# Three edits to a decoder step built from seven-product matmuls: the last four pairs in turns, a norm in single steps, one more weight in flight

## The chip, the cores and the metric

The kernel runs on one core of a Trainium2 chip. The metric is device time in microseconds (us) of one execution. Engines: TensorE (PE; PEld is its weight load), VectorE (DVE), ScalarE (ACT), GpSimd (POOL) and SyncE (SP), which here only issues DMAs.

## The reference

One step of a two-layer decoder, 1,024 prompt positions and 8 single decode positions, width 2048, all in float32. The first layer is a pooling mixer, the second an attention over a window of 128 with shared keys and values. Cut to what matters:

```
def pool_layer(x, ...):                          # layer A
    z = x @ w_in                                 # stage ai: 2048 x 4096
    u, gate = z[..., :D_POOL], z[..., D_POOL:]
    d = grouped_linear(multiscale_pool(u)) * scale
    y = (d * silu(gate)) @ w_out                 # stage ao: 2048 x 2048
    return layer_norm(ALPHA * x + y, g_ln, b_ln)

k, v = shared_kv(h, pos, w_kv)                   # 2048 x 512, from the output of A

def attn_layer(x, ...):                          # layer B
    z = x @ w_in                                 # stage bi: queries and gate, 2048 x 4096
    o = attn_core(rope(q), kb, vb, ..., sinks)   # 32 heads of 64, 4 key/value heads
    y = (o * silu(gate)) @ w_out                 # stage bo: 2048 x 2048
    return layer_norm(ALPHA * x + y, g_ln, b_ln)
```

`layer_norm` takes mean and variance over the 2048 channels of each position.

## The kernel before, in words

Channels lie on the partitions (16 tiles of 128) and positions along the free dimension. The positions are cut into two chunks, the first of 512, the second of 512 + 8 = 520. Each of the four matmuls is run for both chunks, so there are eight stages: ai 0, ai 1, ao 0, ao 1, bi 0, bi 1, bo 0, bo 1 (the table `PHASES`). The sixth is bi 1, which begins with the keys and values of the second chunk; the eighth and last is bo 1, from about 2107 us to 2296 us.

Nearly all matmul work is done in *pairs* of output tiles. A pair is a 2 x 2 block product and takes seven products in place of eight (`seven`), so a stage of 2048 outputs has 8 pairs and 56 products. Each product is 8 steps over the contraction with three matmuls each (lines 684 to 686): a float32 operand is split into a high and a low part, and high x high, high x low and low x high are summed. A product needs one combined weight of 128 x 1024. It is loaded by SP (L285, 512 KB), cast to its high part by ScalarE (L505), and its low part is what VectorE subtracts (L520). The activations go the same way (L828 load, L838 cast, L847 subtraction). Behind each product VectorE or ScalarE takes the sums out of PSUM (L623 to L657).

The order of instructions on an engine is the order in which Python issues them. `begin`, ahead of each product, loads, prepares and casts the weights that lie `self.ahead` products ahead (three numbers: loads, casts, subtractions); `at(n, go)` puts a step behind the n-th product from now; `product(n, ...)` does that for extra matmuls. Side work, such as a norm, is a generator in `self.side`; `end` runs its next step once in `self.every` products if at least `self.room` tiles are free. All tiles come from one pool of 54 (`Mem`); a load into a tile waits for whatever used it before, and SP issues strictly in order.

Names in the prediction: `ln_gen` is the norm of a finished chunk as side work. In the eighth stage it is the last norm of the first chunk (output `y0`): two J sums (matmuls with a constant matrix that add over channels, L952), then for each of the 8 pairs a load (L994), a subtraction of the mean (L1068), a multiplication (L1069), two affine steps on ScalarE (L1060) and a store (L1061). In the sixth stage's transition, L1728 are four transfers that bring partner rows for the rotation, and L657 copies the last product out of PSUM to free it.

`phase_end` is the end of the last stage. The pairs named in `SPLIT` are not worked one behind the other but in turns, product by product, as the table `TAIL` says; `steps` lists what is done behind which product. The second chunk is halved in positions: Bh (260 columns) has its sums of squares and its statistics (`stats`) before the last product, A after it. For each pair, `less` and `rest` build the residual, `square` and `add` feed the sums, `affine1` (L1474, L1478 on VectorE) and `affine2` (L1485 on ScalarE, L1486 the store, output `y1`) finish a half pair, and `back` loads a pair that had been put away. Half A is finished in another way: `turn` transposes the unfinished pairs (L1588), the mean and bias come in as a small matmul (`last_rows`, L1596), and `evict` scales by the row's factor (L1608 on VectorE, L1613 on ScalarE) and stores (L1609, output `y1a`). `sums_a` (L1533) and `sums_z` (L1541) are the final sums, the second of the last pair alone.

Of the kernel before, what the change touches and what calls it, by code (L numbers as in the profile page):

```python
# [66 lines left out]
SPLIT = 5, 6, 7  # L67
TAIL = (
    (5, 0), (5, 2), (5, 1), (6, 0), (5, 3), (5, 4), (6, 2), (6, 1), (7, 0), (6, 3), (7, 2), (7, 1), (6, 4),
    (7, 3), (7, 4), (5, 5), (5, 6), (6, 5), (6, 6), (7, 5), (7, 6),  # L70
# [120 lines left out]
class Kern:  # L191
# [789 lines left out]
    def ln_gen(self, c, pre, acc, gc, bc, out, td):  # L981
# [81 lines left out]
        for p in range(10):  # L1063
            load(p + 2)
            if p < 8:
                t = self.pair_view(pre[p], T)
                if c == 0:
                    nc.vector.tensor_sub(t, t, b2(mu))  # L1068
                nc.vector.tensor_mul(t, t, b2(rr))  # L1069
# [334 lines left out]
    def phase_end(self, c, xs, x_in, pre, acc, gc, bc, out):  # L1404
# [30 lines left out]

        def square(p, h, j=slice(0, 2)):
            if p not in q:
                q[p] = self.mem.full(2 * T)
            nc.scalar.activation(self.pair_view(q[p], T)[:, j, h], tv(p)[:, j, h], AF.Square)

        def add(p, h):
            nc.vector.tensor_add(av[:, :, h], av[:, :, h], tv(p)[:, :, h])
            nc.vector.tensor_add(qv[:, :, h], qv[:, :, h], self.pair_view(q[p], T)[:, :, h])

        def sums(h):
# [3 lines left out]
            for ps, a, w in zip(R[h.start], (av, qv), (tv(z), self.pair_view(q[z], T))):  # L1449
                srcs = [v[:, j, h] for v in (a, w) for j in range(2)]  # L1450
# [3 lines left out]
        def stats(h):  # L1454
# [4 lines left out]
            nc.scalar.copy(m, mb[:, :TH])  # L1459
            nc.vector.tensor_mul(qq, m, m)  # L1460
# [76 lines left out]
        def sums_z(n):  # L1537

            w = (tv(z), self.pair_view(q[z], T))[n]
            for j in range(2):  # L1540
                nc.tensor.matmul(  # L1541
                    R[0][n][:, :TH], J, w[:, j, A], start=False, stop=j == 1, skip_group_check=True,
                )

        def moments():
# [15 lines left out]
            affine1a(1, Bh)  # L1561
# [7 lines left out]
            affine1b(1, Bh)  # L1569
# [32 lines left out]
        def evict(b, k):  # L1602
# [3 lines left out]
            r = box["rc"][:, b : b + 1]  # L1606
            if k % 2:
                nc.vector.tensor_scalar(y, X[b, k][:], r, None, op0=ALU.mult)  # L1608
# [3 lines left out]
            else:  # L1612
                nc.scalar.activation(y, X[b, k][:], AF.Copy, scale=r)  # L1613
# [13 lines left out]
        x, y, z = SPLIT  # L1627
        for p in SPLIT:
            box, z0, z1 = self.two(T)

            def open_(p=p, box=box, z0=z0):
# [6 lines left out]
            (x, 0): [lambda: x_in(y)],  # L1638
            (x, 2): [lambda: less(x)],
            (y, 0): [lambda: x_in(z)],  # L1640
# [22 lines left out]
            (z, 5): [lambda: square(y, A), lambda: affine(x, Bh), lambda: spare(4), lambda: scale(4)],  # L1663
            (z, 6): [
                lambda: square(z, A, 0), lambda: add(y, A), lambda: scale(z, (0,), True),
            ],
        }
        for p, idx in TAIL:
            for go in steps.get((p, idx), []):
                self.at(0, go)  # L1670
            if (p, idx) == (x, 5):
# [13 lines left out]
        scale(y)  # L1685
        spare(y)
        spare(z)
        affine1(z, Bh)
# [25 lines left out]
        affine1(3, Bh)  # L1714
        affine2(2, Bh)
# [766 lines left out]
```

## Time and profile before

| | |
|---|---|
| median of 3 runs | 2322.99 us (2320.79 to 2325.85) |
| profiled execution | 2320.17 us |
| its span, first to last instruction | 2317.9 us |
| TensorE busy | 2288.1 us, 99% |
| VectorE, ScalarE, GpSimd busy | 84%, 60%, 8% |
| mean granted TensorE clock | 0.997 |
| HBM traffic over the span | 275 GB/s |

The profiled execution takes 2.3 us outside its span. The page gives the busy time of each engine, groups of instructions by line, and the chain of work that ended last; the trace behind it answers what an engine waited for and what each did in any stretch. A releaser named behind an idle time is inferred, and of several it is the one that came last.

### The profile page before, as it was taken

The numbers are of one execution on the slowest core, as the hardware profiler recorded it, in microseconds if no ns is written. First come the engines' busy times: TensorE is split into PE (matmuls) and PEld (weight loads), VectorE is DVE, ScalarE is ACT, GpSimd is POOL, SyncE is SP. The second block draws the span as 40 slices with busy tenths as digits, with TensorE's granted clock in tenths as the row PEclk, the third lists the DMA queues.
The fourth block names the chain that finished last, engine by engine and source line by source line (L and its number), as shares of the span: only waits on it lengthen the run. The fifth ranks groups of instructions, "written<-read, shape, count | busy, mean of one in ns | idle before, by whom it ended". The sixth has DMA issues, their size and how long they took to land. (4 is left out here: it accounts for less than half of the span.)

```text
span 2317.9 us, 50529 instructions
## 1 busy us (share of the span) xinstructions
PE 2288.1 (99%) x20417; PEld 2217.7 (96%) x20417; DVE 1943.0 (84%) x2409; ACT 1389.3 (60%) x2548; POOL 191.1 (8%) x360
## 2 busy tenths in 40 slices
PE   9999999999999999999999999999999999999997
PEld 7999999999999999999889999989999999999997
DVE  8888889877878878988979898889877777889797
ACT  5544446544546547655566767685776678556565
POOL 0111110010000000000001111100000000000001
PEclk9999999999999999999999999999999999999999
DMA  7869679999989989999767666777787878799795
GB/s 261 287 242 315 229 245 330 315 309 303 304 302 322 335 284 333 317 392 345 245 234 241 233 234 236 252 259 250 234 252 240 252 230 288 251 360 381 252 330 184
DMA packets 246682, 649.37 MB, mean 280 GB/s; under 512 B 25232, under 2 KB 106032, under 8 KB 246448
## 3 DMA queue, kind: packets, MB, share of 16 engines
q1 hardware_dynamic: 204432, 493.66, 63.8%
q0 software_dynamic: 42016, 152.49, 17.0%
q8 instruction: 159, 2.61, 0.5%
q14 instruction: 75, 0.61, 0.1%
HBM read 463.54 MB, written 173.01 MB: 275 GB/s over the span
## 5 line engine op out<-in xcount | busy, mean ns | idle before, releaser
L684 PE MATMUL pD<-m,m 128*128 128x260 f32 (+1 forms) x5088 | 1441.3, 283 | 4.7 <-ACT pD L623 2.3
L686 PE MATMUL pD<-m,m 128*128 128x260 f32 (+1 forms) x5088 | 1434.7, 282 | 4.9 <-DVE m L520 4.9
L685 PE MATMUL pD<-m,m 128*128 128x260 f32 (+1 forms) x5088 | 1434.7, 282 | 0.0
L684 PEld LDWEIGHTS pD<-m,m 128*128 128x128 f32 x5088 | 959.4, 189 | 13.9 <-issue 6.2
L686 PEld LDWEIGHTS pD<-m,m 128*128 128x128 f32 x5088 | 959.8, 189 | 7.1 <-DVE m L520 7.0
L685 PEld LDWEIGHTS pD<-m,m 128*128 128x128 f32 x5088 | 959.1, 189 | 0.5
L520 DVE TENSOR_TENSOR m<-m,m 128x1024 fp32r<-128x1024 f32 x690 | 833.5, 1218 | 94.7 <-ACT m L505 44.1
L505 ACT CAST m<-m 128x1024 fp32r<-128x1024 f32 x690 | 720.5, 1049 | 249.9 <-DVE m L349 120.3
L349 DVE TENSOR_TENSOR m<-m,m 128x1024 f32<-128x1024 f32 x136 | 166.1, 1222 | 10.2 <-DMA m<-in_wia 5.7
L847 DVE TENSOR_TENSOR m<-m,m 128x1024 fp32r<-128x1024 f32 (+1 forms) x118 | 143.8, 1224 | 7.4 <-ACT m L838 5.8
L838 ACT CAST m<-m 128x1024 fp32r<-128x1024 f32 (+1 forms) x118 | 123.3, 1051 | 11.8 <-DVE m L520 3.5
L657 ACT COPY m<-pD 128x260 f32<-128x260 f32 (+1 forms) x89 | 33.2, 373 | 131.0 <-PE pD L686 131.0
L645 DVE TENSOR_TENSOR m<-pD,m 128x260 f32<-128x260 f32 (+1 forms) x92 | 38.4, 418 | 73.1 <-ACT pD L644 67.2
L1910 ACT ACTIVATE m<-m,sm 128x128 f32<-128x128 f32 x256 | 99.4, 392 | 0.0
L623 ACT ACTIVATE pD<-pD 128x260 f32<-128x260 f32 (+1 forms) x90 | 33.3, 370 | 102.2 <-PE pD L686 102.0
L1179 PE MATMUL pD<-m,m 128*128 128x260 f32 (+1 forms) x528 | 91.5, 323 | 0.0
L712 PE MATMUL pD<-m,m 128*128 128x512 f32 x224 | 89.1, 398 | 0.0
L714 PE MATMUL pD<-m,m 128*128 128x512 f32 x224 | 88.2, 394 | 0.0
L713 PE MATMUL pD<-m,m 128*128 128x512 f32 x224 | 88.1, 393 | 0.0
L1179 PEld LDWEIGHTS pD<-m,m 128*128 128x128 f32 x528 | 79.4, 188 | 8.2
L1923 ACT ACTIVATE m<-m,sm 128x128 f32<-128x128 f32 x256 | 81.8, 391 | 3.8 <-DVE sm L1918 3.4
L632 ACT COPY m<-pD 128x260 f32<-128x260 f32 (+1 forms) x92 | 34.3, 373 | 82.3 <-PE pD L686 82.0
(257 smaller groups left out, 2101.3 us busy)
## 6 DMA issues: line engine op xcount, KB each, us to landing
m<-in_wib SPq DMA_DIRECT2D x132, 512.0 KB
m<-in_wia SPq DMA_DIRECT2D x128, 512.0 KB
m<-swoa SPq DMA_DIRECT2D x64, 512.0 KB
swia<-m POOLq DMA_DIRECT2D x56, 512.0 KB, 4.9
m<-swia SPq DMA_DIRECT2D x56, 512.0 KB
m<-swob SPq DMA_DIRECT2D x56, 512.0 KB
m<-in_wob SPq DMA_DIRECT2D x52, 512.0 KB
m<-in_woa SPq DMA_DIRECT2D x48, 512.0 KB
```

Of the source, the lines that this page charges most:

```text
L349: self.nc.vector.tensor_add(s[out].a[:, :1024], s[x].a[:, :1024], s[y].a[:, :1024])
L505: self.nc.scalar.copy(hi.r[:, :1024], self.stream[self.cast].src().a[:, :1024])
L520: self.nc.vector.tensor_sub(lo.r[:, :1024], s.src().a[:, :1024], hi.a[:, :1024])
L684: nc.tensor.matmul(ps[:, :TH], wh[:, s], h, start=new and k == 0, stop=False, skip_group_check=on)
L685: nc.tensor.matmul(ps[:, :TH], wh[:, s], l, start=False, stop=False, skip_group_check=on)
L686: nc.tensor.matmul(ps[:, :TH], wl[:, s], h, start=False, stop=k == 7, skip_group_check=on)
L712: nc.tensor.matmul(ps[:], wh[:, s], h, start=par == 0 and k == 0, stop=False)
L714: nc.tensor.matmul(ps[:], wl[:, s], h, start=False, stop=par == 1 and k == 7)
L838: self.nc.scalar.copy(h.r[:, :n], s.a[:, :n])
L847: self.nc.vector.tensor_sub(l.r[:, :n], s.a[:, :n], h.a[:, :n])
L1179: nc.tensor.matmul(ps[:, : cs.stop - cs.start], ws[:, s], d[:, cs], start=f0 and k == 0, stop=l0 and k == 3,)
L1910: nc.scalar.activation(x["s3"][:, i, :], x["s3"][:, i, :], AF.Exp, bias=nm[:, i : i + 1], scale=0.125, accum_out=rs[:, i : i + 1],)
```

## The change

It has three parts.

1. `SPLIT` takes in pair 4 and `TAIL` grows from 21 to 28 products. Squares get tiles of half a pair, freed as soon as they are added. Three reloads (`back`) instead of four. The affine steps of the pairs 4, 1, 2, 5 and 3 on half Bh are spread behind products of the last turns; behind the last product only those of the pairs 6 and 7 and the last part of pair 3 are left. `evict` is told its engine.
2. In `ln_gen`, the step that held a subtraction and a multiplication becomes two steps for the `y0` norm, and in the eighth stage `self.every` goes from 2.75 to 1.5.
3. In the last pair of bi 0, `self.ahead` becomes 8, 4, 3 and, 30 products later, 7, 4, 3 again.

```
-SPLIT = 5, 6, 7
+SPLIT = 4, 5, 6, 7
 TAIL = (
-    (5, 0), (5, 2), (5, 1), (6, 0), (5, 3), (5, 4), (6, 2), ...
+    (4, 0), (4, 2), (4, 1), (5, 0), (4, 3), (4, 4), (5, 2), ...
...
                 if c == 0:
                     nc.vector.tensor_sub(t, t, b2(mu))
+                    if td is None:
+                        yield
                 nc.vector.tensor_mul(t, t, b2(rr))
...
         def square(p, h, j=slice(0, 2)):
-            if p not in q:
-                q[p] = self.mem.full(2 * T)
-            nc.scalar.activation(self.pair_view(q[p], T)[:, j, h], tv(p)[:, j, h], AF.Square)
+            if (p, h.start) not in q:
+                q[p, h.start] = self.mem.half(T)
+            nc.scalar.activation(qh(p, h)[:, j], tv(p)[:, j, h], AF.Square)
...
-            (z, 3): [lambda: rest(y, Bh), lambda: square(y, Bh), lambda: back(1), lambda: back(2)],
+            (z, 3): [lambda: rest(y, Bh), lambda: square(y, Bh), lambda: back(1)],
             (z, 4): [
-                lambda: add(y, Bh), lambda: rest(y, A), lambda: back(3), lambda: back(4),
+                lambda: add(y, Bh), lambda: rest(y, A), lambda: back(2), lambda: back(3),
                 lambda: spare(0), lambda: scale(0),
             ],
-            (x, 6): [
-                lambda: stats(Bh), lambda: spare(1), lambda: scale(1), lambda: spare(2), lambda: scale(2),
-            ],
-            (y, 5): [
-                lambda: square(x, A), lambda: affine(0, Bh), lambda: spare(3), lambda: scale(3),
-            ],
-            (y, 6): [
-                lambda: add(x, A), lambda: rest(z, A), lambda: spare(x), lambda: scale(x),
-            ],
-            (z, 5): [lambda: square(y, A), lambda: affine(x, Bh), lambda: spare(4), lambda: scale(4)],
+            (w, 6): [lambda: stats(Bh), lambda: spare(1), lambda: scale(1)],
+            (x, 5): [lambda: square(w, A), lambda: affine(0, Bh), lambda: spare(2), lambda: scale(2)],
+            (x, 6): [lambda: add(w, A), lambda: spare(w), lambda: scale(w)],
+            (y, 5): [lambda: square(x, A), lambda: affine(w, Bh), lambda: spare(3), lambda: scale(3)],
+            (y, 6): [lambda: add(x, A), lambda: affine(1, Bh), lambda: spare(x), lambda: scale(x)],
+            (z, 5): [lambda: square(y, A), lambda: affine(2, Bh), lambda: affine1(x, Bh)],
             (z, 6): [
-                lambda: square(z, A, 0), lambda: add(y, A), lambda: scale(z, (0,), True),
+                lambda: square(z, A, 0), lambda: add(y, A), lambda: scale(z, (0,), True), lambda: scale(y),
+                lambda: spare(y), lambda: affine1(3, Bh), lambda: affine2(x, Bh),
             ],
...
-        affine2(z, Bh)
+        affine2(3, Bh)
         last_rows(0, range(4))
         last_rows(1, range(3))
-        affine1(2, Bh)
-        for k in range(4):
-            evict(0, k)
-        last_four()
-        affine2(1, Bh)
+        evict(0, 0, False)
+        evict(0, 1, True)
+        evict(0, 2, True)
+        affine2(z, Bh)
         X[1, 3] = self.psD()
         turn(1, 12, 16)
         last_rows(1, (3,))
-        affine1(3, Bh)
-        affine2(2, Bh)
-        for k in range(4):
-            evict(1, k)
-        affine1(4, Bh)
-        affine2(3, Bh)
-        affine2(4, Bh)
+        evict(0, 3, True)
+        last_four()
+        evict(1, 0, False)
+        evict(1, 1, True)
+        evict(1, 2, False)
+        evict(1, 3, True)
...
             if p == ps[-1]:
                 self.x_begin(nxt)
                 if c == 1:
                     self.ahead = 6, 4, 3
+                else:
+                    self.ahead = 8, 4, 3
+                    self.at(30, lambda: setattr(self, "ahead", (7, 4, 3)))
...
             elif (kind, c) == ("bo", 1):
                 gen = self.ln_gen(0, *acc[0], C_GB, C_BB, io["y0"], None)
                 self.at(3, lambda gen=gen: add("y", gen))
-                self.every, self.room = 2.75, 3
+                self.every, self.room = 1.5, 3
```

In the kernel after the change the lines behind 1068 have numbers two to eight higher (L1474 is L1481 there, L1608 is L1615, L1728 is L1732).

How the order of instructions moves is shown at two places. The first is SP's queue at the begin of the sixth stage: `in_wib` are weights of the stage's matmul, `in_wkv` those of keys and values, `h` and `th` the activations and their sums. Before:

```order
L285 DMA m_1957_17713<-in_wib 128x1024
L285 DMA m_1963_17786<-in_wib 128x1024
L285 DMA m_1974_17956<-in_wib 128x1024
L828 DMA m_1979_18002<-h_95 128x4x260
L828 DMA m_1989_18088<-th_92 128x4x260
L1728 DMA m_1977_17995<-m_1962_17784 32x1024 x4
L828 DMA m_1978_18000<-h_95 128x4x260
L285 DMA m_1980_18006<-in_wkv 128x1024
L828 DMA m_1983_18044<-h_95 128x4x260
L828 DMA m_1984_18046<-h_95 128x4x260
L285 DMA m_1986_18050<-in_wkv 128x1024
```

After, from the same place on:

```order
L285 DMA m_1955_17675<-in_wib 128x1024
L285 DMA m_1960_17744<-in_wib 128x1024
L285 DMA m_1975_17958<-in_wkv 128x1024
L285 DMA m_1970_17912<-in_wib 128x1024
L285 DMA m_1991_18093<-in_wkv 128x1024
L828 DMA m_1979_18002<-h_95 128x4x260
L1732 DMA m_1978_17997<-m_1963_17786 32x1024 x4
L828 DMA m_1980_18004<-h_95 128x4x260
L285 DMA m_1981_18008<-in_wkv 128x1024
L828 DMA m_1984_18046<-h_95 128x4x260
L828 DMA m_1985_18048<-h_95 128x4x260
L285 DMA m_1987_18052<-in_wkv 128x1024
```

Two `in_wkv` loads have moved ahead of the first `h` load and of the four partner transfers (L1728, now L1732); the `th` load has moved behind these transfers and five more loads, to the place behind the last row.

The second is VectorE behind the last product, from the last half of an affine multiplication on (L1478, now L1485) to the kernel's end. L1553 (now L1560) makes the last factors, L1608 (now L1615) is an eviction. Before:

```order
L1478 TENSOR_TENSOR m_3046_28333<-m_3046_28333,m_3058_28452 128x2x260
L1553 TENSOR_TENSOR m_3065_28648<-m_3064_28647,m_3065_28648 32x256 x2
L1474 TENSOR_TENSOR m_3047_28335<-m_3047_28335,m_3058_28452 128x2x260
L1478 TENSOR_TENSOR m_3047_28335<-m_3047_28335,m_3058_28452 128x2x260
L1608 TENSOR_SCALAR m_3068_28701<-pD_28628,sm_28687 128x512
L1608 TENSOR_SCALAR m_3069_28705<-pD_28638,sm_28687 128x512
L1474 TENSOR_TENSOR m_3051_28372<-m_3051_28372,m_3058_28452 128x2x260
L1478 TENSOR_TENSOR m_3051_28372<-m_3051_28372,m_3058_28452 128x2x260
L1608 TENSOR_SCALAR m_3070_28728<-pD_28670,sm_28687 128x512
L1608 TENSOR_SCALAR m_3071_28732<-pD_28717,sm_28687 128x512
L1474 TENSOR_TENSOR m_3052_28374<-m_3052_28374,m_3058_28452 128x2x260
L1478 TENSOR_TENSOR m_3052_28374<-m_3052_28374,m_3058_28452 128x2x260
```

After, from the same instruction on:

```order
L1485 TENSOR_TENSOR m_3022_28091<-m_3022_28091,m_3055_28395 128x2x260
L1560 TENSOR_TENSOR m_3068_28671<-m_3067_28670,m_3068_28671 32x256 x2
L1615 TENSOR_SCALAR m_3071_28722<-pD_28651,sm_28710 128x512
L1615 TENSOR_SCALAR m_3072_28726<-pD_28660,sm_28710 128x512
L1615 TENSOR_SCALAR m_3072_28726<-pD_28661,sm_28710 128x512
L1615 TENSOR_SCALAR m_3073_28744<-pD_28693,sm_28710 128x512
L1615 TENSOR_SCALAR m_3074_28748<-pD_28731,sm_28710 128x512
```

The subtractions and multiplications of three half pairs have gone from behind the final factors to places further ahead, and five evictions stand there instead of four.

More of the change, by code (lines that the diff above doesn't have):

```diff
@@ L1434, in rest, with qh @@
             nc.vector.tensor_add(tv(p)[:, :, h], tv(p)[:, :, h], x[:, :, h])
+        def qh(p, h):
+            return q[p, h.start].a[:, : 2 * TH].rearrange("p (k t) -> p k t", k=2)
         def square(p, h, j=slice(0, 2)):
[L1437 to L1439 removed]
+            if (p, h.start) not in q:
+                q[p, h.start] = self.mem.half(T)
+            nc.scalar.activation(qh(p, h)[:, j], tv(p)[:, j, h], AF.Square)
         def add(p, h):
             nc.vector.tensor_add(av[:, :, h], av[:, :, h], tv(p)[:, :, h])
[L1443 removed]
+            nc.vector.tensor_add(qv[:, :, h], qv[:, :, h], qh(p, h))
+            q.pop((p, h.start)).free()
         def sums(h):
@@ L1448, in sums @@
             z = SPLIT[-1]
-            for ps, a, w in zip(R[h.start], (av, qv), (tv(z), self.pair_view(q[z], T))):
-                srcs = [v[:, j, h] for v in (a, w) for j in range(2)]
+            for ps, a, w in zip(R[h.start], (av, qv), (tv(z)[:, :, h], qh(z, h))):
+                srcs = [v[:, j] for v in (a[:, :, h], w) for j in range(2)]
                 for i, v in enumerate(srcs):
@@ L1459, in stats @@
             nc.scalar.copy(m, mb[:, :TH])
+            rest(z, A)
             nc.vector.tensor_mul(qq, m, m)
@@ L1600, in last_rows, with evict @@
                 )
-        def evict(b, k):
+        def evict(b, k, dve):
             if k % 2 == 0:
@@ L1637, in phase_end @@
         steps = {
-            (x, 0): [lambda: x_in(y)],
-            (x, 2): [lambda: less(x)],
-            (y, 0): [lambda: x_in(z)],
+            (w, 0): [lambda: x_in(x)],
+            (w, 2): [lambda: less(w)],
+            (w, 4): [lambda: less(x), lambda: x_in(y)],
+            (x, 2): [lambda: rest(w, Bh)],
+            (x, 1): [lambda: square(w, Bh)],
+            (y, 0): [lambda: add(w, Bh)],
+            (x, 3): [lambda: rest(w, A), lambda: x_in(z)],
             (x, 4): [lambda: less(y)],
```

26 lines of the change are left out of this document (12 added, 14 removed).

## The prediction

> **What bounds the kernel now.** I read the page's engine table first, then the waits of TensorE, then each of the places that the diff touches in the windows and the timeline.
>
> ```profile
> span 2317.9 us, 50529 instructions
> PE 2288.1 (99%) x20417; PEld 2217.7 (96%) x20417; DVE 1943.0 (84%) x2409; ACT 1389.3 (60%) x2548; POOL 191.1 (8%) x360
> ```
>
> TensorE is busy for 99% of the span, and the change adds or removes no matmul of a product. So only time in which TensorE stands still or runs slowly, and the 11 us or so behind the last product, can be won: 2317.9 - 2288.1 = 29.8 us in all. The waits of TensorE say where the standing still is.
>
> ```profile
> PE pD L672 <- ACT m L657: 4.9, 1, 4.9
> ...
> PE pD L684 <- ACT m L657: 1.6, 1, 1.6
> ```
>
> Columns: what waited for what, us in total, times, the longest. The first row is one wait, three times as long as the next longest single one, the second row. It lies at the begin of the sixth stage (second chunk's bi), where the third part of the change acts. The windows there show that it costs twice, once as idle time and once in the clock:
>
> ```profile
> 1504.00:1508.00 4.00, 2.68 (x23) 1.00 1.05 375
> ...
> 1512.00:1516.00 4.00, 4.00 (x20) 0.50 1.05 389
> ```
>
> The columns are the TensorE busy time (and matmuls), the granted clock, the DMA engines' share and GB/s. TensorE stops 2.68 us into the first of them, at 1506.68. Behind the wait the clock is 0.50, and only 20 matmuls start in 4 us. The DMA engines are full throughout. What TensorE waited for is on ScalarE, and what ScalarE waited for is in the queue of SP:
>
> ```profile
> 1500.47 0.36 ACT L644 COPY pD<-pD 128x256 f32<-128x256 f32 x1
> 1504.33 1.05 ACT L505 CAST m<-m 128x1024 fp32r<-128x1024 f32 x1 [3.49 <-DVE m L1960]
> ...
> 1511.17 0.37 ACT L657 COPY m<-pD 128x256 f32<-128x256 f32 x1
> ```
>
> ```profile
> 1480.71 0.38 SPq L828 DMA_DIRECT2D m<-h  x1
> 1487.73 0.38 SPq L828 DMA_DIRECT2D m<-th  x1
> 1488.20 3.11 SPq L1728 DMA_DIRECT2D m<-m  x4
> ...
> 1492.73 0.59 SPq L285 DMA_DIRECT2D m<-in_wkv  x1
> ...
> 1494.83 2.16 SPq L285 DMA_DIRECT2D m<-in_wkv  x3
> ```
>
> ScalarE stood for 3.49 us before the cast of a weight (L505). The row names a VectorE step, but that step had begun at 1503.4 on work unrelated to the tile; I read it as the landing of the second in_wkv load, issued at 1494.83 and queued behind full DMA engines. From 1504.33 on ScalarE works without a gap up to L657, which frees TensorE. SP issued nothing between 1481.1 and 1487.7: a th load stood at its head and waited for its tile. Everything behind it, the in_wkv weights too, came 6.6 us late, and then all at once.
>
> **The change part by part.** *Weights 8 ahead.* It is one assignment, worth one more weight that may be in flight before the pair ends. By the order of SP the first two in_wkv loads now stand before the h load of 1480.71 and before the partner transfers (L1728), and the th load has gone behind them. So the two weights that came too late are issued some 12 us earlier, before the blocked place and not behind it. The L505 of 1504.33 can then begin at 1500.83, when L644 ends, and the unbroken work behind it (1511.17 - 1504.33 = 6.84 us) ends in an L657 that starts at 1507.67 and ends at 1508.04. TensorE would wait from 1506.68 to 1508.1, 1.4 us instead of 4.92: **3.5 us** won. Now the clock:
>
> ```profile
> 1505.81 0.28 PE L684 MATMUL pD<-m,m 128*128 128x256 f32 x1
> 1505.93 0.28 PE L685 MATMUL pD<-m,m 128*128 128x256 f32 x1
> ...
> 1511.60 1.02 PE L672 MATMUL pD<-m,m 128*128 128x260 f32 x3 [4.92 <-ACT m L657]
> ...
> 1517.39 0.32 PE L686 MATMUL pD<-m,m 128*128 128x260 f32 x1
> ```
>
> Before the wait a matmul starts every 0.12 us. Between the rows of 1511.60 and 1517.39 27 start in 5.79 us, which at that pace would take 3.24: **2.6 us** lost (2.55). Behind the wait of 1.6 us quoted above the clock did not fall, so a wait of 1.4 should cost nothing more. Between 1.6 and 4.9 us the trace shows nothing. The Trainium skill ("TensorE: Matmul & The Clock Gate", section "What's actually happening") says that the clock halves after at least one idle window of about 3.4 us and is given back after one busy window of that length. The trace agrees on the halving, but the clock stayed low for some 6.7 us, twice that; by the page's figure the loss would be about 1.7 us in place of 2.6, and the sum 0.9 us smaller.
>
> Bounds for this part: if all 4.92 us go, 7.5 us; if the wait only passes to another load, nothing. The later slots of tiles and the sums of weights (L453 and following) shift a little all through this stage; VectorE has 4 of 8 us idle right behind the transition, so I put that at 0, with 2 us either way in the range.
>
> *First chunk's last norm in single steps, asked for at 1.5 instead of 2.75.* No work is added; eight pairs of one subtraction and one multiplication, and the two J sums before them, move forward in the eighth stage. In before the last of these multiplications starts at 2262.8 (row below), the first subtraction 59 us ahead of it; in after's order the first subtraction stands where before had 2172, and the last pair about 15 us earlier than it did.
>
> ```profile
> L1069 DVE TENSOR_TENSOR m<-m,m x24: 1224/1226/1235, 949.0 to 2262.8; 128x1024 f32<-128x1024 f32 x16, 128x1040 f32<-128x1040 f32 x8
> ```
>
> ```profile
> 2140.00:2150.00 10.00, 10.00 (x10) 1.00 0.95 363
> 2150.00:2160.00 10.00, 6.87 (x9) 1.00 0.80 268
> 2160.00:2170.00 10.00, 7.37 (x10) 1.00 0.79 270
> 2170.00:2180.00 10.00, 6.61 (x7) 1.00 0.57 170
> 2180.00:2190.00 10.00, 9.62 (x11) 1.00 0.92 297
> 2190.00:2200.00 10.00, 7.48 (x8) 1.00 0.61 210
> ```
>
> Columns: VectorE busy, clock, DMA share, GB/s. VectorE is idle for 12.05 us of 2150 to 2200. Counted along after's order, with each instruction at its duration in before, VectorE has done 1.4 us more than before at 2154, 4.7 more at 2172, 8.2 at 2191 and at most 9.8 at 2217. The idle time up to those points is 1.3 us or more, 6, 11 and 12, so it fits, barely at 2154: two operations of 1.2 us now stand ahead of an L520 there while VectorE is fully booked, which I put at 0.5 us of TensorE's time. The same holds for the DMA engines: three loads and two stores of 0.52 MB come before 2195, 2.6 MB or 7 us at 370 GB/s, where 13 us of their time is free. In return the crowded stretch of 2200 to 2264 is relieved, with its last wait of 0.8 us at 2268. Together **0.3 us** won, from 1 us won to 1.5 lost.
>
> *Four pairs in turns.* The products stay 56, in another order. Pair 4 joins the turns; affine steps of four half pairs leave the end and go ahead of the last product; one reload of a pair goes away.
>
> ```profile
> L1608 DVE TENSOR_SCALAR m<-pD,sm 128x512 f32<-128x512 f32 x4 | 2.8, 744 | 0.0
> L1478 DVE TENSOR_TENSOR m<-m,m 128x520 f32<-128x520 f32 x4 | 2.8, 700 | 0.1
> ```
>
> ```profile
> 2306.28 0.99 SPq L1609 DMA_DIRECT2D out_y1a<-m  x2
> ...
> 2310.83 2.46 SPq L1486 DMA_DIRECT2D out_y<-m  x2
> ```
>
> ```profile
> 2300.00:2310.00 10.00, 5.42 (x39) 4.53 (x37) 9.70 (x18) 8.31 (x17) 1.49 (x3) 0.97 0.46 169
> 2310.00:2318.00 8.00, 0.00 (x0) 0.00 (x0) 0.84 (x2) 1.23 (x3) 0.00 (x0) 0.50 0.72 255
> ```
>
> The evictions (L1608 on VectorE) and the affine pairs (L1474, L1478) take turns behind the last product; the last stores are issued from 2310.83 on, and the span ends at 2317.9. From 2307 on the stores stand in a queue: 8 us x 255 GB/s = 2.0 MB go out in the last window. After the change three half pairs of 0.27 MB fewer are stored behind the final sums, 0.8 MB or 2.2 us at 370 GB/s, and the first y1a store, at 2306.28 before, comes about 0.5 us sooner because two evictions now run at once on ScalarE and VectorE. That is 2.7 us won, if the queue of stores stays the bound. VectorE's own end would allow more: three affine pairs of 1.4 us leave it there, 4.2 us, and one eviction of 0.7 comes.
>
> The four pairs must be done earlier, 4 x 1.4 = 5.6 us. Is there room?
>
> ```profile
> 2280.00:2290.00 10.00, 7.51 (x13) 1.00 0.64 228
> 2290.00:2296.00 6.00, 4.17 (x8) 1.00 0.19 67
> ```
>
> ```profile
> 2296.13 0.43 DVE m L655
> ```
>
> ```profile
> 2295.93 1.92 PE L1533 MATMUL pD<-m,jr 128*128 128x260 f32 x8
> 2297.68 1.92 PE L1541 MATMUL pD<-m,jr 128*128 128x260 f32 x8
> ```
>
> VectorE is idle for 2.5 + 1.8 us there, so it does not quite fit. Walking after's order behind the seventh last product, at these durations, the last L655 starts 1.8 us after the last product instead of at once. TensorE's own sums (L1533) cover 1.75 us; the rest, with the latencies, delays L1541 by 0.7. So the end brings 2.7 - 0.7 = **2.0 us**, from 0.5 to 4.
>
> **The sum.** 3.5 + 2.6 + 0.3 + 2.0 = 8.4 us. Against the profiled execution's 2320.17 us (span 2317.9 and 2.3 around it) that is 2311.8; the median of the runs lies 2.8 above the profiled one, so the forecast in their terms is 2322.99 - 8.4 = **2314.6 us**.
>
> **The rivals.** *The wait of the sixth stage stays, wholly or long enough for the clock.* For it: the DMA engines are full there, the loads are only put in another order, and what frees the tiles of the earlier weights cannot be seen in the order. Against it is the stretch ahead, with a DMA share of 0.39, in which the loads have room to go out earlier:
>
> ```profile
> 1468.00:1480.00 12.00, 12.00 (x173) 11.44 (x172) 9.03 (x11) 7.85 (x21) 1.92 (x4) 1.00 0.39 136
> ```
>
>  If the wait falls to 3.5 us and the clock still halves, 1.4 + 0.3 + 2.0 = 3.7 us are won: 2319.3, which a measurement cannot tell from no change. If it stays wholly, 2320.7. Chance 0.17. By the skill's rule above, a wait of 3.4 us is about the border; I take the border from the trace as anywhere between 1.6 and 4.9.
>
> *The norm's loads and stores block SP in the eighth stage (slower).* A store of y0 (L1061) stands in SP's queue until ScalarE has finished its affine, with the weights behind it; five such transfers now stand before 2195 that were behind. The place at 1481 prices one block: 6.6 us of silence on SP became 4.92 us of idle TensorE and 2.6 us of clock, 7.5 together. It bites only where a block exceeds the lead of a weight's load over its cast:
>
> ```profile
> 2165.53 3.19 SPq L285 DMA_DIRECT2D m<-in_wob  x2
> ```
>
> ```profile
> 2178.62 1.07 ACT L505 CAST m<-m 128x1024 fp32r<-128x1024 f32 x1
> ```
>
> This cast reads the first of the two tiles, 13 us after its issue; with some 3 us for the transfer, a block of up to 10 us would not show. Two blocks beyond that, at the price above, cost 15 us: 2314.6 + 15 = 2329.6. Against it, such a lead is usual in this stage. Chance 0.15.
>
> *The end gives nothing back*, because VectorE is later by more than the 1.8 us: then 2316.6 or a little more, still faster; chance 0.08, and it lies in the range.
>
> **How the numbers follow.** The forecast has 0.60. About 0.2% (4.6 us) is what a measurement of this kernel can tell from no change. Faster by more than that: 0.60 and the 0.08 of a lost end, 0.68. Within it: 0.17. Slower: 0.15. The forecast's own range runs from 2310 (7.5 us at the sixth stage, 4 at the end, 1 in between) to 2318; to leave out no more than 2 in 10 it has to take in the first rival, with a measurement's spread of 2 to 3 us on top, to 2323.5. The slower rival stays outside.
>
> **What would show it.** Right: no TensorE wait over 2 us between 1500 and 1515 and no clock below 1.0 there; in_wkv loads issued before 1482; SP silent later, if at all; in the eighth stage no new TensorE wait over 1 us; a last y1 store issued some 4 us earlier behind the last L1553, and the last L655 some 1.5 us behind the last product. Wrong: a wait of L672 on L657 that is still over 3 us, a clock of 0.5 anywhere behind the start, or waits on L520 of over 2 us between 2140 and 2270.

## The result and the profile after

| kernel | median of its runs | ratio to before, 95% interval |
|---|---|---|
| before | 2323.14 us (2319.91 to 2325.85, 6 runs) | |
| after | 2309.90 us (2306.85 to 2311.31, 6 runs) | 0.9944 [0.9931, 0.9956] |

The change takes 13.2 us off by the medians, 13 by the ratio (10 to 16); 8.4 were forecast, and the time stands at the lower end of the forecast's own range, 2310. The profiled execution of after took 2311.31 us with a span of 2308.8, 9.1 less than the span of before. Its page, and its waits of TensorE:

```profile
span 2308.8 us, 50518 instructions
...
PE 2286.2 (99%) x20417; PEld 2216.1 (96%) x20417; DVE 1943.5 (84%) x2415; ACT 1389.0 (60%) x2547; POOL 191.1 (8%) x359
```

```profile
PE pD L686 <- DVE m L520: 5.8, 8, 2.5
...
PE pD L684 <- ACT m L657: 1.7, 1, 1.7
...
PE pD L672 <- ACT m L657: 0.5, 1, 0.5
```

The wait of 4.9 us on L657 is down to 0.5. A new one stands in the first row: of eight waits on L520 the longest is now 2.5 us, where before had 0.9.

Both traces have 5,152 matmuls of line 684, so the n-th of one can be set beside the n-th of the other. The difference of their starts says where the time went:

| place | before | after | difference |
|---|---|---|---|
| ahead of the wait in the sixth stage (n = 3232) | 1500.73 | 1500.20 | -0.5 |
| behind it and the low clock (3256) | 1518.35 | 1510.85 | -7.5 |
| late in the seventh stage (4440) | 2032.97 | 2025.00 | -8.0 |
| near its end (4616) | 2096.41 | 2091.34 | -5.1 |
| last turns of the eighth (5112) | 2281.31 | 2275.68 | -5.6 |
| end of the last product | 2296.09 | 2290.23 | -5.9 |
| end of the span | 2317.9 | 2308.8 | -9.1 |

So the sixth stage brought 7.0 us, the end of the seventh took 2.9 back, the eighth brought 0.8 and what lies behind the last product 3.2.

**The sixth stage.** The windows of TensorE (busy, clock, DMA share, GB/s), then ScalarE's and SP's timeline there:

```profile
1504.00:1508.00 4.00, 3.54 (x29) 1.00 1.05 380
...
1512.00:1516.00 4.00, 4.00 (x36) 1.00 1.07 382
```

```profile
1497.39 0.38 ACT L644 COPY pD<-pD 128x256 f32<-128x256 f32 x1
1498.78 1.05 ACT L505 CAST m<-m 128x1024 fp32r<-128x1024 f32 x1 [1.01 <-DVE m L520]
...
1506.19 0.37 ACT L657 COPY m<-pD 128x256 f32<-128x256 f32 x1 [0.45 <-PE pD L686]
```

```profile
1467.99 0.33 SPq L285 DMA_DIRECT2D m<-in_wkv  x1
...
1479.92 0.33 SPq L285 DMA_DIRECT2D m<-in_wkv  x1
1480.52 0.46 SPq L828 DMA_DIRECT2D m<-h  x1
1482.50 2.94 SPq L1732 DMA_DIRECT2D m<-m  x4
...
1491.80 0.73 SPq L828 DMA_DIRECT2D m<-th  x1
```

The clock is 1.00 and 36 matmuls start in the window that had 20. L657 now waits for the last product and not for ScalarE's own work. L644 ran at 1497.39 and not at 1500.47, though TensorE was only 0.5 us ahead: ScalarE had been late before its long wait already. Two rows of before say how that came about, a store of GpSimd and a cast of ScalarE:

```profile
1481.09 0.55 POOL L1963 DMA_DIRECT2D o<-m  x1 [1.22 <-DVE m L895]
```

```profile
1497.28 1.06 ACT L838 CAST m<-m 128x1040 fp32r<-128x1040 f32 x1 [2.66 <-DMA m<-h]
```

The semaphores in the trace tell when a transfer has landed. The store landed at 1487.59, SP waited for its semaphore ahead of the th load, and that load left at 1487.73. So the tile that the load was to fill was still being stored. The h load that the cast needs stood behind the th load too. It was issued at 1491.41 and landed at 1497.26, so 2.66 us were lost ahead of L644, before the 3.49 us that the prediction shows. Those ended as it read them, with the landing of the second in_wkv load at 1504.26.

In after the two in_wkv loads left at 1468 and 1480, the partner transfers 5.7 us earlier than in before.

**Behind the last product.** The stores and the final sums, with VectorE's last product eviction (L655), then the last two windows of the span:

```profile
2299.96 0.34 SPq L1619 DMA_DIRECT2D out_y1a<-m  x1
2300.60 0.37 SPq L1493 DMA_DIRECT2D out_y<-m  x1
2301.24 2.34 SPq L1619 DMA_DIRECT2D out_y1a<-m  x3
```

```profile
2290.07 1.92 PE L1540 MATMUL pD<-m,jr 128*128 128x260 f32 x8
2291.82 1.92 PE L1548 MATMUL pD<-m,jr 128*128 128x260 f32 x8
```

```profile
2291.59 0.42 DVE L655 TENSOR_TENSOR m<-pD,m 128x260 f32<-128x260 f32 x1
```

```profile
2300.00:2304.00 4.00, 0.87 (x6) 0.52 (x4) 2.53 (x4) 1.73 (x4) 0.00 (x0) 1.00 0.84 298
2304.00:2308.80 4.80, 0.00 (x0) 0.00 (x0) 0.00 (x0) 0.00 (x0) 0.00 (x0) 0.64 0.63 250
```

L655 starts 1.36 us behind the last product, and L1548 follows L1540 after 1.75 us, exactly as L1541 followed L1533 in before: the lateness lies wholly under the first sums. Nothing is issued behind 2303.6, while in before the last two y1 stores were issued from 2310.83 on.

### The profile page after: what moved, and what is told of

Its sections match the earlier page's. It is cut to its first block, busy times and chain, and to the rows that moved or that the text cites. A ratio compares the mean times of both kernels' runs of the same rounds, so it can differ in the third digit from the quotient of the medians.

```text
span 2308.8 us, 50518 instructions
## 1 busy us (share of the span) xinstructions
PE 2286.2 (99%) x20417; PEld 2216.1 (96%) x20417; DVE 1943.5 (84%) x2415; ACT 1389.0 (60%) x2547; POOL 191.1 (8%) x359
## 3 DMA queue, kind: packets, MB, share of 16 engines
q8 instruction: 159, 2.61, 0.5%
## 4 chain that ended last, share of the span: by engine, by line
PE 56%; DVE 1%; DMA 1%; ACT 0%; issue 0%; POOL 0%; SPq 0%; DVEq 0%; POOLq 0%
PE pD L684 15%; PE pD L686 14%; PE pD L685 14%; PE pO L1955 2%; PE pD L712 2%; PE pD L714 2%; PE pD L713 2%; PE pS L1878 2%; PE pS L1931 1%; DMA m<-in_wob 0%; PE pS L1955 0%; PE pO L684 0%; PE pO L685 0%; PE pO L686 0%; DVE m L520 0%; DMA m<-in_wib 0%
## 5 line engine op out<-in xcount | busy, mean ns | idle before, releaser
L520 DVE TENSOR_TENSOR m<-m,m 128x1024 fp32r<-128x1024 f32 x690 | 834.1, 1219 | 94.4 <-ACT m L505 37.9
L505 ACT CAST m<-m 128x1024 fp32r<-128x1024 f32 x690 | 720.6, 1049 | 247.5 <-DVE m L349 122.4
L657 ACT COPY m<-pD 128x260 f32<-128x260 f32 (+1 forms) x88 | 32.9, 374 | 125.8 <-PE pD L686 125.6
L632 ACT COPY m<-pD 128x260 f32<-128x260 f32 (+1 forms) x92 | 34.4, 374 | 82.6 <-PE pD L686 82.4
```

Of the source, the lines that this page charges most:

```text
L505: self.nc.scalar.copy(hi.r[:, :1024], self.stream[self.cast].src().a[:, :1024])
L520: self.nc.vector.tensor_sub(lo.r[:, :1024], s.src().a[:, :1024], hi.a[:, :1024])
```

## The experiments

All times are medians; the ratios are to runs of before on the same chip.

| kernel | median, us | ratio | TensorE's wait in the sixth stage, us | span behind the last product, us |
|---|---|---|---|---|
| third part alone | 2313.12 | 0.9962 [0.9950, 0.9974] | 0.46 | 22.0 |
| second part alone | 2319.55 | 0.9988 [0.9979, 0.9997] | 5.25 | 22.0 |
| first and second part | 2316.95 | 0.9977 [0.9968, 0.9986] | 4.75 | 18.3 |
| before, th load moved | 2317.16 | 0.9975 [0.9965, 0.9984] | 1.87 | 22.3 |
| before, second trace | | | 4.59 | 22.3 |
| after, again | 2309.88 | 0.9955 [0.9942, 0.9969] | 0.46 | 18.3 |

**The three parts.** The third alone:

```
             if p == ps[-1]:
                 self.x_begin(nxt)
                 if c == 1:
                     self.ahead = 6, 4, 3
+                else:
+                    self.ahead = 8, 4, 3
+                    self.at(30, lambda: setattr(self, "ahead", (7, 4, 3)))
```

> Only the third part: one more weight in flight at the begin of the sixth stage. Theory A (all the gain of the sixth stage comes from this part, and some of it is given back where the DMA engines are full, near 2085 us): the wait of TensorE for L657 falls from 4.9 to under 1 us and the clock stays at 1.0, 7.5 us won by 1520; a wait for L520 of about 2.5 us with a halved clock behind it near 2085, where before had 0.9, so some 3 us back; 4 to 6 us won in all. Theory B (the wait near 2085 comes from another part of the change): 7 to 8 us won, and no wait over 1.2 us near 2085.

It was 8.8 us faster (6 to 11.6). The trace has the wait of 0.46 us and no low clock there, and the difference of the starts goes from +1.1 to -5.9 across the place (n = 3232 to 3256): 7.0 us, as in after. Near 2085 there is no wait over 0.4 us, and nothing is given back. The figures are those of theory B, but not its reason: up to the eighth stage the instructions of this kernel and of after stand in the same order, so the wait at 2085 in after's trace comes neither from this part nor from another. What the place does in other traces is said below.

The second alone (the diff of `ln_gen` and of `self.every`):

> Only the second part: the first chunk's last norm in single steps, at 1.5. Theory A: 0.5 to 1.5 us won by the last product (the two small waits of 0.2 and 0.8 us at 2265 to 2268 go), nothing anywhere else, which is too little to be told by the times. Theory B (the earlier steps of the norm crowd VectorE, and the gain of the whole change stands in spite of them): 1 us or more lost between 2140 and 2220.

2.8 us faster by the ratio (0.7 to 4.9). By the trace it stands 1.1 us behind the first trace of before at n = 4616, shortly ahead of the eighth stage, and ends the last product 0.5 us ahead of it; the waits at 2265 to 2268 are gone. 1.6 us is a little above theory A, inside the interval of the times. Theory B fails.

The first two together, which is the change without its third part:

> The first two parts without the third. Theory A: the wait of 4.9 us at the begin of the sixth stage and the clock of 0.5 behind it are as in before; no wait over 1.2 us near 2085 to 2093; 0.8 us won by the norm and 3.2 behind the last product, 4 in all. Theory B (the wait near 2085 does not hang on the sixth stage): a wait of about 2.5 us near 2093, and only some 1 us won in all.

5.3 us faster (3.2 to 7.4), with the wait of 4.75 us and the low clock in the sixth stage, and 1.19 us near 2092. The span behind the last product is 3.5 us shorter than in before's first trace. Theory A in its signs; the time came out above its 4 us, inside the interval. With the third part's 8.8 this makes 14.1, and the whole change has 13 (10 to 16): the parts add up. The first part, as the difference of this kernel and the one before it, is 2.6 us by the medians.

**What held the weights up.** In before, SP's loads at the begin of the sixth stage are put in the order of the source, still 7 ahead (`SPAN` holds two positions in the list of instructions, taken at the first h load of the stage and one product into it):

```
-    for i in tc.nc.cur_bb.bb.instructions:
-        if i.engine in ENGINES:
+    for n, i in enumerate(tc.nc.cur_bb.bb.instructions):
+        if i.engine in ENGINES or i.engine == mybir.EngineType.SP and SPAN[0] <= n < SPAN[-1]:
```

> Before with one load put elsewhere: at the begin of the sixth stage SP issues its loads in the order of the source, so that the th load stands behind the partner transfers and two in_wkv loads; still 7 weights in flight. Theory A (the th load at the head of SP's queue, waiting for its tile, made the weights late): the wait for L657 falls below 2 us, no clock of 0.5 behind it, 5 to 7.5 us won at the sixth stage. Theory C (it is the number of weights in flight, the th load only happened to stand there): the wait stays at 3 us or more with the halved clock, and 0 to 2 us are won.

5.8 us faster (3.7 to 8.1). The edit moves the th load behind the partner transfers, three h loads and two in_wkv loads, and swaps two of the h loads; nothing else. SP's timeline, ScalarE's (L508 and L660 are the casts and the copy, L505 and L657 in before) and the windows:

```profile
1483.16 4.90 SPq L1733 DMA_DIRECT2D m<-m  x4
1488.15 0.53 SPq L833 DMA_DIRECT2D m<-h  x1
1488.86 0.44 SPq L288 DMA_DIRECT2D m<-in_wkv  x1
1489.34 0.98 SPq L833 DMA_DIRECT2D m<-h  x2
1490.36 0.67 SPq L288 DMA_DIRECT2D m<-in_wkv  x1
1491.19 3.25 SPq L833 DMA_DIRECT2D m<-th  x1
```

```profile
1501.40 1.05 ACT L508 CAST m<-m 128x1024 fp32r<-128x1024 f32 x1 [2.98 <-DVE m L648]
...
1508.26 0.36 ACT L660 COPY m<-pD 128x256 f32<-128x256 f32 x1
```

```profile
1504.00:1508.00 4.00, 2.80 (x24) 1.00 1.07 383
1508.00:1512.00 4.00, 3.33 (x27) 1.00 1.05 390
1512.00:1516.00 4.00, 4.00 (x37) 1.00 1.05 389
```

The partner transfers leave 5 us earlier, the in_wkv loads 4 us; ScalarE still waits 2.98 us for the second of them, TensorE 1.87 us in place of 4.92, and the clock stays at 1.00. Theory A holds for the larger part: one blocked load at the head of the queue was worth 5.6 us across the place by the starts (from +0.1 to -5.5) of the 7.0 that the third part brings. For the rest, 1.4 us, the weight had to be in flight still earlier: by its semaphore, the load issued at 1490.36 landed at 1501.33, and the cast began at 1501.40.

**What differs between executions.** Before and after, each once more:

> The kernel before once more, for a second trace. The first one was of an execution of 2320.2 us, below the median of its runs. Theory A (the forecast was read from a quick execution, and a usual one loses more where the DMA engines are full): one or more waits of TensorE of 1 to 3 us that the first trace does not have, and a span of 2319 us or more. Theory B (what lies between executions is spread evenly over many small waits): the same list of waits within 0.5 us.

> The changed kernel once more. Its first trace has a wait of 2.5 us for L520 at 2085 with a halved clock behind it; the kernel with the third part alone, whose instructions stand in the same order up to there, had none. Theory A (chance of one execution): no wait over 1.3 us near 2085 here, the last product 2 to 3 us earlier than in the first trace. Theory B (the change brings it): the wait of 2 us or more is there again.

Before's second trace spans 2319.8 us. Its waits:

```profile
PE pD L686 <- DVE m L520: 5.8, 9, 1.6
PE pD L672 <- ACT m L657: 4.6, 1, 4.6
PE pD L684 <- ACT m L632: 1.7, 1, 1.7
```

The wait on L632 near 2269 is 1.7 us and not 0.8, one at 1500 is 1.4 and not 0.2: theory A, in small pieces. After, measured again beside other runs of before, was 10.4 us faster by the ratio (7.2 to 13.5). Its second trace spans 2306.4, 11.5 us below before's first; the waits, and the windows of TensorE at 2085:

```profile
PE pD L686 <- DVE m L520: 5.3, 10, 1.1
```

```profile
2083.00:2085.00 2.00, 1.99 (x17) 1.00 0.90 276
2085.00:2087.00 2.00, 1.25 (x10) 1.00 1.04 413
2087.00:2089.00 2.00, 2.00 (x19) 1.00 1.03 417
```

In the first trace of after the same place reads

```profile
2085.00:2087.00 2.00, 0.00 (x0) 0.96 1.03 407
2087.00:2089.00 2.00, 1.67 (x8) 0.50 1.04 399
```

```profile
2083.43 0.43 DVE L895 TENSOR_TENSOR m<-m 128x260 f32<-128x260 f32 x1 [2.61 <-DMA m<-o]
```

There VectorE stood 2.61 us for a load of side work (sums for the eighth stage) with the next weight's L520 queued behind it. Theory A as to the size, 2.46 us once and 0.77 the other time, with the DMA engines full in both. The place itself returns: the kernel with smaller stores (below), in the same order up to there, waited 1.90 us at it, and the traces of before and of the other kernels so far 0.4 to 1.6.

**Two places where time seemed left.** In after, side steps every 2 products in the seventh stage (`self.every = 2` under `("bo", 0)`), and, in another kernel, SP in the order of the source at the begin of that stage:

> The changed kernel with side steps every 2 products instead of 3 in the seventh stage, so that the last of the sums for the eighth stage, whose loads VectorE waited for at 2083 in the first trace of after, are no longer forced behind one another at that stage's end. Theory A (the wait at 2085 is a matter of chance in some executions): 0 to 1.5 us faster than the changed kernel by the median, no wait over 1 us between 2080 and 2095. Theory B (the wait is there in most executions): 2.5 us or more faster. Theory C: VectorE and the DMA engines are full there, and the earlier steps only move the wait forward; 0 or slower.

> The changed kernel with SP's loads in the order of the source at the begin of the seventh stage, where an in_wob load stood at SP's head for 4.3 us ahead of the partner transfers and a weight (in_wib) that ScalarE then waited for. Theory A (the same mechanism as at the sixth stage's begin: a blocked load ahead of those that are needed sooner): the wait of 1.7 us for L657 near 1944 falls below 0.7, 1 to 1.5 us faster than the changed kernel. Rival: the wait stays, since there ScalarE has more work than time (it is without a gap for the last 7 us ahead of that L657); within 0.5 us of the changed kernel.

The first took 2308.49 us (0.9948 [0.9936, 0.9961]), 1.4 us under the repeated after, with overlapping intervals; no wait over 0.4 us at 2085. Theory A. The eleven traces without this edit all have a wait there, of 0.4 to 2.5 us; the two with it have none over 0.3. So the edit does take it away, but what that is worth the times do not tell. The second took 2311.05 us (0.9960 [0.9947, 0.9972]), no gain. The load that stood at SP's head moved back, but the wait near 1944 stayed:

```profile
PE pD L687 <- ACT m L660: 2.4, 1, 2.4
```

```profile
1929.76 1.05 ACT L508 CAST m<-m 128x1024 fp32r<-128x1024 f32 x1 [1.94 <-DMA m<-in_wib]
```

Theory A fails, and the time is nearer to the rival: 1.2 us above the repeated after, with overlapping intervals. The rival's reason, ScalarE's own work, is not shown: ScalarE waited for the same in_wib weight as without the edit, and then twice more for in_wob weights (1.57 and 0.47 us).

**What sets the end.** Before without three of the stores behind the last product, and after with smaller stores:

```
-            nc.sync.dma_start(out[:, 2 * p : 2 * p + 2, :], t)
+            if p not in (2, 3, 4) or h.start == 0:
+                nc.sync.dma_start(out[:, 2 * p : 2 * p + 2, :], t)
```

> The kernel before without the stores of half Bh of the pairs 2, 3 and 4 to y1, 0.27 MB each, which it issues behind the last product; their affine steps stay. So three parts of one output are not written. Theory A (the end is bound by the queue of stores): the span behind the last product, 21.6 us in before, shrinks by about 2 us, 0.8 MB at 370 GB/s. Theory B (the end is bound by the steps of VectorE and ScalarE, and the last stores come when these are done): the last y1a store is issued at the same distance from the last product, and lands at most 2.2 us sooner than the last y1 store did only because that one is gone; what is issued stays at the same times, and DMA share after 2310 falls without the first y1a store landing earlier.

This kernel leaves out three parts of an output. It took 2319.54 us (0.9984 [0.9975, 0.9994]), 3.7 us less. The span behind the last product is 19.0 us in place of 22.1, the mean of the five traces that end as before does (21.8 to 22.3; in before's first it is 21.8 and not 21.6). Stores are issued up to 2312.8:

```profile
2309.13 0.99 SPq L1610 DMA_DIRECT2D out_y1a<-m  x2
2310.21 0.56 SPq L1487 DMA_DIRECT2D out_y<-m  x1
2311.79 1.02 SPq L1610 DMA_DIRECT2D out_y1a<-m  x2
```

The last product ended at 2298.94 here, so the last y1a store goes out 13.5 us behind it, against 14.0 in before: the issue has hardly moved, and 3.1 us are gone all the same. That is the size of theory A, but it has a sign of theory B too: the first y1a store landed at the same distance, 12.8 us. The landings tell the two apart. All times are in us behind the last product; the step is the last one of VectorE or ScalarE whose result is stored:

| trace | last step ends | last store issued | landed | span ends |
|---|---|---|---|---|
| before | 15.9 | 16.0 | 20.7 | 21.8 |
| before without three stores | 13.5 | 13.5 | 17.7 | 19.0 |
| after | 12.3 | 12.4 | 17.4 | 18.5 |
| after, smaller stores | 12.3 | 14.9 | 18.7 | 19.6 |

In before a y1 store issued at 5.5 us, with no other close to it, landed 2.6 us later; the last stores of the table need 3.8 to 5.0. So the queue holds some 1 to 2.5 us of the end, and the rest is when the last store can leave. Without the three stores the last landing is 3.0 us earlier: 2.1 because no y1 store lands behind the last y1a one any more (18.7 and 20.7 in before), 0.5 because that one leaves sooner and 0.5 because it lands faster. In before SP issues without a pause from 11.2 us on and is done with the store ahead of the last one just when the last step ends, so there both bind; in after SP waits for the last evictions.

```
-            if k % 2:
-                nc.sync.dma_start(
-                    io["y1a"][b * P : (b + 1) * P, (k - 1) * 512 : (k + 1) * 512], Y[b, k // 2].a[:, :1024]
-                )
+            nc.sync.dma_start(io["y1a"][b * P : (b + 1) * P, k * 512 : (k + 1) * 512], y)
```

> The changed kernel with each eviction stored by itself (0.26 MB as soon as it is evicted) in place of two together. Theory A (what is left of the end is bound by when the evictions are done, since the DMA share is 0.84 and 0.63 in the last two windows): the first store leaves some 0.7 us sooner, the last lands 0.3 to 1 us sooner. Theory B (the eight issues on SP and the queue cost as much as they bring): the same span behind the last product within 0.3 us, or longer.

The end took 19.6 us, 1.1 more than the 18.5 of the five traces that end as after does (18.3 to 19.0), though the first store left sooner; by the times 2310.06, no different. Theory B: SP issued the eight one behind the other, the last 2.5 us behind its eviction.

> The changed kernel with both: side steps every 2 products in the seventh stage and each eviction stored by itself. If the two small gains are real, 1.5 to 2.5 us faster than the changed kernel; if they are not, within 1 us of it.

2308.34 us, 0.9935 [0.9920, 0.9951]: 1.5 us under after, and not to be told from it. Its end took 19.7 us, so the smaller stores lengthen it here too. None of these is shown to beat the change.

## Why the prediction was right, and where it was too small

*Sixth stage, forecast 3.5 + 2.6 us.* The cause held: a th load at SP's head, the in_wkv weights behind it, ScalarE, then TensorE, then the clock. The kernel with that load alone moved shows it. The sum was 6.1 and the starts give 7.0, in after and in the third part alone. Against the five traces that have the wait the gain is 5.5 to 7.3, 6.5 in the mean. The step that was mis-sized is the remaining wait, put at 1.4 us and measured at 0.46: the chain of 6.84 us behind L644 was left where it stood, but L644 itself had been held up by some 3 us, most of it by the h load that stood behind the th load as well. With only the load moved the remaining wait was 1.87.

*The clock.* 2.6 us, and it came: no low clock in the sixth stage in any kernel with the third part. That a wait of 1.4 us costs nothing more was not put to the test, since 0.46 remained; 1.87 us in the kernel with the load moved cost nothing. The term is less fixed than the prediction had it: of the five traces with the wait three have the clock low for 6.8 us and two for 3.4, before's second among these. The prediction's sentence by the Trainium skill ("TensorE: Matmul & The Clock Gate", section "What's actually happening") has the clock given back after one busy window of about 3.4 us. Both executions agree with it if a window that begins with TensorE still idle does not count as busy: TensorE was idle for 0.95 us of the first low window in before's first trace and for 0.02 in its second. The last section has the working.

*The norm, 0.3 us.* Its room was rightly read. The eighth stage's VectorE, in after:

```profile
2150.00:2160.00 10.00, 6.07 (x10) 1.00 0.92 333
2160.00:2170.00 10.00, 9.93 (x12) 1.00 0.68 224
...
2250.00:2260.00 10.00, 5.58 (x7) 1.00 0.79 289
```

The busy share has moved forward, and no wait over 0.4 us came of it. It moved further than was counted: the last pair's subtraction starts at 2228.3 and not at 2261.6, of which 5 us are what after is ahead, and the prediction had 15. From the seventh stage's end to the last product after's first trace gains 0.8 us, its second 0, the second part alone 1.6. The times put that part at 2.8 (0.7 to 4.9). Over all traces, from n = 4616 to the end of the last product the five with the norm as in before take 199.9 us in the mean (199.4 to 200.6) and the eight with the new one 199.1 (198.1 to 200.0). So the step is worth some 0.8 us, and the term was too small by 0.5. About 0.6 of it shows in one wait, TensorE's longest on L632 in that stretch: 0.5 to 1.7 us in those five, 0.4 or none in seven of the eight.

*The end, 2.7 - 0.7 us.* It brought 3.2 in the traces compared and 3.6 over all of them (22.1 against 18.5). Two steps failed. The 0.7 did not come: the last L655 is 1.36 us late and not 1.8, and so stays under the 1.75 us of TensorE's first sums. And the 2.7 took the queue of stores for the bound. In the five traces that end as before does the last step of VectorE and ScalarE ends 15.9 us behind the last product, in the five that end as after does 12.3; the last store leaves within 0.3 us of it and needs 4.7 to 5.2 us to land, before and after. So the end moved with the steps, by 3.6 us. The prediction had that figure, 4.2 - 0.7 = 3.5 for VectorE's own end, and set it aside.

*The rivals.* A wait in the sixth stage that stays: refuted. SP blocked in the eighth stage by the norm's stores: no TensorE wait over 0.4 us there. An end that gives nothing: refuted. One of the prediction's signs of being wrong did appear, a clock of 0.50 behind the start: for 3.4 us from 2086.9 in the first trace of after. It belongs to the wait at 2085, for which the forecast had no term and which the second trace has at 0.77 us with the clock at 1.00.

*What remains of 13.2 against 8.4.* The means over all traces give 6.5 (sixth stage), 0.8 (norm) and 3.6 (end), 10.9 in all. That lies inside the interval of both measurements, 13 (10 to 16) and 10.4 (7.2 to 13.5), so 2.5 us of the difference are found, most of them at the end. Whether the other 2 are more than the spread of the times is not shown. The profiled execution of before was a quick one, 2.8 us under the median of its runs, and the prediction moved the difference over to the median as if it stayed there. That the first two traces differ by 9.1, so near to the 8.4, is luck in part: the terms brought more, and the wait at 2085 took 2.9 back.

## What to carry to other kernels

Where one queue issues strictly in order, look for a stretch of silence in it and then for what stood at its head: one load that could not go yet had made SP, ScalarE and TensorE late one behind the other. A wait of the engine that bounds the kernel is to be priced with the clock behind it, and the chain behind the wait is to be followed back further than the last idle row, since its begin may be late as well. One profiled execution is one draw: a wait of 2.5 us in the first trace of after was 0.8 in the second and 1.9 in a third kernel with the same order. And a load that left late is to be followed to its landing: here the semaphores said which store had blocked the queue, and that the end hung on the last step and not on the queue alone.

## What the runs showed of the hardware

The clock fell to 0.50 behind far shorter waits than had been seen in the first trace. Two rows of the windows, of after with side steps every 2 products, behind a wait of 1.90 us, and of the second part alone, behind one of 2.34:

```profile
1948.00:1950.00 2.00, 2.00 (x12) 0.54 1.05 385
```

```profile
1954.00:1956.00 2.00, 2.00 (x19) 1.00 1.05 379
```

Behind waits of 1.90, 2.36, 2.46 and 2.56 us the clock was low for 3.4 us; behind others of 1.87, 1.90, 2.05 and 2.34 it did not fall; behind those of 4.6 to 5.5 us it was low for 3.4 or 6.8. So between 1.9 and 2.5 us the length of a wait does not say whether it costs the clock.

What does is where the wait lies. Every stretch of constant clock in the thirteen traces, but for the last, lasts a whole number of times 3.413 us: 1505.28 us is 441 of them, 6.83 two, 3.41 one. The first begins 4.3 to 6.9 us behind the start of the span, at another place in each trace. So the clock is set in steps of 3.41 us that do not follow the kernel, and each trace can be cut into these windows. The idle time of TensorE in them:

| trace | wait, us | idle in the windows that it touches, us | clock in the window behind |
|---|---|---|---|
| after, side steps every 2 | 1.90 | 1.90 | 0.50 |
| after, smaller stores | 1.90 | 0.39 and 1.50 | 1.00 |
| before, th load moved | 1.87 | 1.30 and 0.57 | 1.00 |
| first and second part | 2.05 | 0.62 and 1.43 | 1.00 |
| second part alone | 2.34 | 1.47 and 0.87 | 1.00 |
| after, first trace | 2.46 | 1.99 and 0.47 | 0.50 |
| after, first trace, at 1943 | 1.72 | 1.72 | 1.00 |

In all thirteen traces the clock fell behind every window with 1.90 us or more of idle time, and behind none with 1.72 or less. Behind a window at the low clock it came back where TensorE had been idle for at most 0.58 us of it, and stayed low for one window more where it had been 0.95 or more; this is what makes 3.4 or 6.8. What lies between these figures no trace shows. By these figures a wait of up to 1.7 us costs only itself where no other idle time shares its window; of a longer one it hangs on where it falls, and the longest that went free here is 2.34 us.
